# Every fourth weight chunk's lower half made by ScalarE and an adding transfer

## The chip, the cores and the metric

One core of one Trainium2 chip. The metric is the device time of one execution in microseconds. The core has a matrix engine (TensorE, PE in the profile, with its weight loads as PEld), a vector engine (VectorE, DVE), an activation engine (ScalarE, ACT), GpSimd (POOL) and SyncE (SP). Transfers run on 16 DMA engines; SP, ACT and POOL issue them from queues of their own.

## The reference

A small decoder trunk over 256 tokens of width 2048 in float32: one layer with a dilated-mixture attention, one layer with a gated sum of compressed, selected and windowed attention, and in each layer an MLP of width 8192 and a gated embedding branch. Cut to the top:

```python
for i in range(DEPTH):                      # DEPTH = 2
    hn = rmsnorm(h, attn_norm_g[i])
    if i < N_A_LAYERS:
        h = h + dilated_mixture_attention(hn, a_w_in[i], a_w_out[i])
    else:
        shared = nsa_shared_kv(rmsnorm(h, kv_norm_g), w_kv_shared, ...)
        h = h + nsa_attention(hn, b_w_qg[j], b_w_out[j], *shared)
    hn = rmsnorm(h, mlp_norm_g[i])
    h = h + jnp.square(jax.nn.relu(hn @ mlp_w1[i])) @ mlp_w2[i]
    gate = jax.nn.sigmoid(rmsnorm(h, ple_norm_g[i]) @ ple_w_gate[i])
    h = h + (p[i] @ ple_w_proj[i]) * gate
return rmsnorm(h, final_norm_g)
```

Nearly all of the work is the products with the float32 weight matrices. Each weight is used once, for 256 tokens.

## The kernel before, in words

All weights lie in HBM as *chunks* of 128 partitions by 1024 float32 values, 512 KB each, in the order in which they are used. A float32 product is made of products in float32r, a rounded form that TensorE takes: a weight chunk `raw` is split into `hi` (its rounded copy) and `lo` (what the rounding left), and the activations are split in the same way. One tile of 128 by 128 weights then takes two matmuls (`mm_tile`, lines 319 and 320): `hi` times both halves of the activations (512 columns), and `lo` times the upper half alone (256 columns). A chunk holds eight such tiles.

Where a chunk goes depends on the stage. `quad` (most stages: attention output, MLP, gate, shared keys) collects four output blocks over eight chunks; `single` (queries and keys) collects one block over two chunks; `token_major` (values) uses the weights as the streamed side (lines 402 to 404); `compress` feeds the compression MLP with its chunks interleaved with a value unit's. What comes out of a group is finished by small operations on ScalarE and VectorE: `sum_halves` (lines 324 and 326), `split_to` (430 and 432), `renorm`, `add_to_x` (435 and 436), the softmax of the two attentions.

The order of the work is written out by hand. `Program` holds a list of steps, either a chunk with the function that uses it or a plain operation. `Program.run` goes through the list, and for the chunk `at` it emits, in this order: loads as far as the raw buffers allow (`DMA_AHEAD`, `RAW_BUFS`), rounded copies up to `at + ahead + 1`, subtractions up to `at + ahead`, one step of every operation in progress (`advance`), and then the chunk's matmuls. `ahead` is `SPLIT_AHEAD` after the first chunks. Each engine runs its own instructions in the order in which they were emitted.

Four queues carry the chunk: SyncE issues its load (line 185), ScalarE makes `hi` by a copy that rounds (line 197), VectorE makes `lo = raw - hi` (line 203), TensorE reads both. There are 4 raw, 6 hi and 5 lo buffers; an engine that writes a buffer waits until the last reader of its old contents is done. The very first chunk is handled in two pieces.

GpSimd has little to do: four loads of the per-layer embeddings (`load_p`, line 484), and at the start of layer B, in `start1` (lines 748 to 774), a few memsets and small loads of tables into memory that the earlier layer gives up.

Of the kernel before, what the change touches and what calls it, by code (L numbers as in the profile page):

```python
# [13 lines left out]
ALU = mybir.AluOpType  # L14
# [17 lines left out]

WARM_UP = 7
DMA_AHEAD = 7
SPLIT_AHEAD = 3
RAW_BUFS, HI_BUFS, LO_BUFS = 4, 6, 5

G_ATTN, G_MLP, G_PLE, G_KV, G_FIN = 0, 2, 4, 6, 7

# [1 line left out]
def f32(ap):  # L41
    return ap.bitcast(F32)


class Program:
# [53 lines left out]
    def run(self, load, copy, sub):  # L99
        srcs = [s for s, _ in self.steps if s is not None]  # L100
        raw, hi, lo = {}, {}, {}
        loaded = at = copied = subbed = 0
        for src, fn in self.steps:
            if src is None:
                g = fn()
                if g is not None:
                    self.begin(g)
                continue
            starting = at < KT // 2
            if starting:  # L110
                self.advance()
            ahead = max(0, min(SPLIT_AHEAD, at - KT // 2 + 2))
            while loaded < len(srcs) and loaded <= at + DMA_AHEAD:
                if loaded >= RAW_BUFS and loaded - RAW_BUFS >= subbed:
                    break
                raw[loaded] = load(loaded, srcs[loaded])
                loaded += 1
            while copied < loaded and copied <= at + ahead + (ahead > 0):
                hi[copied] = copy(copied, raw[copied])
                copied += 1  # L120
            while subbed < copied and subbed <= at + ahead:
                lo[subbed] = sub(subbed, raw.pop(subbed), hi[subbed])
                subbed += 1
            if not starting:
                self.advance()
            self.waiting += fn(hi.pop(at), lo.pop(at)) or []
            self.finish_tensor()
            at += 1
        self.until(lambda: not self.active and not self.waiting)
# [3 lines left out]
def kernel(ctx: ExitStack, tc: tile.TileContext, a: dict, out: bass.AP):  # L133
    nc = tc.nc
# [55 lines left out]
    def pieces(n):  # L190

        return [slice(0, CH // 2), slice(CH // 2, CH)] if n == 0 else [slice(0, CH)]
# [4 lines left out]
            nc.scalar.copy(hi[:, c], t[:, c])  # L197
        return hi

    def sub(n, t, hi):  # L200
        lo = wpool.tile([P, CH], F32R, tag="lo", name="wlo", bufs=LO_BUFS)
        for c in pieces(n):
            nc.vector.tensor_sub(lo[:, c], t[:, c], f32(hi)[:, c])  # L203
        return lo
# [928 lines left out]
    ple(1, p1, x_p1, n_p1, None, n_fin, True)  # L1133

    prog.run(load, copy, sub)
    close_pool("h")

# [96 lines left out]
```

## Time and profile before

| | |
|---|---|
| median of two runs | 2530.66 us (2530.20 and 2531.12) |
| profiled execution, first to last instruction | 2529.0 us (the page gives its span only) |
| TensorE busy | 2511.8 us, 99% |
| TensorE weight loads | 2219.4 us, 88% |
| VectorE busy | 1718.4 us, 68% |
| ScalarE busy | 1329.4 us, 53% |
| GpSimd busy | 10.5 us |
| moved by DMA | 466.27 MB, mean 184 GB/s |

The profile is taken from one execution. "Busy" is time in which an engine executes an instruction; weight loads overlap matmuls. A group's row names the line, engine and operation, the tile written and the tiles read, the shapes, the count, then the busy time in us and the mean of one in ns, and after a second bar the idle time of the engine just before these instructions with what ended it. In the rows of waits, the name left of the arrow waited for the one right of it; `mm` and `at` are TensorE's two sets of result banks. A DMA issue row ends with the median time from issue to landing.

### The profile page before, as it was taken

The numbers are of one execution on the slowest core, as the hardware profiler recorded it, in microseconds if no ns is written. First come the engines' busy times: TensorE is split into PE (matmuls) and PEld (weight loads), VectorE is DVE, ScalarE is ACT, GpSimd is POOL, SyncE is SP. The second block draws the span as 40 slices with busy tenths as digits, with TensorE's granted clock in tenths as the row PEclk, the third lists the DMA queues.
The fourth block names the chain that finished last, engine by engine and source line by source line (L and its number), as shares of the span: only waits on it lengthen the run. The fifth ranks groups of instructions, "written<-read, shape, count | busy, mean of one in ns | idle before, by whom it ended". The sixth has DMA issues, their size and how long they took to land.

```text
span 2529.0 us, 38529 instructions
## 1 busy us (share of the span) xinstructions
PE 2511.8 (99%) x14717; PEld 2219.4 (88%) x14717; DVE 1718.4 (68%) x3035; ACT 1329.4 (53%) x2066; POOL 10.5 (0%) x22
## 2 busy tenths in 40 slices
PE   9999999999999999999999999999999999999997
PEld 7888888888888888888888899988888888888887
DVE  6766677866566565566788988766656656556777
ACT  6444444564354453455665777655435445445555
POOL 0000000000000000000000000000000000000000
PEclk9999999999999999999999999999999999999999
DMA  7555555566666666666566743456666666666653
GB/s 262 175 175 178 174 164 179 175 187 189 191 191 191 188 190 190 191 191 189 183 199 189 254 150 114 134 188 187 190 190 191 191 188 189 190 191 191 189 186 118
DMA packets 129690, 466.27 MB, mean 184 GB/s; under 512 B 14560, under 2 KB 15328, under 8 KB 129504
## 3 DMA queue, kind: packets, MB, share of 16 engines
q1 hardware_dynamic: 128112, 461.50, 59.2%
q8 instruction: 115, 1.88, 0.3%
q0 software_dynamic: 528, 1.07, 0.2%
q10 hardware_dynamic: 864, 1.25, 0.1%
q14 instruction: 71, 0.58, 0.1%
HBM read 461.65 MB, written 2.10 MB: 183 GB/s over the span
## 4 chain that ended last, share of the span: by engine, by line
PE 99%; DVE 0%; DMA 0%; ACT 0%; issue 0%; ACTq 0%; DVEq 0%
PE mm L319 29%; PE at L319 26%; PE mm L320 15%; PE at L320 13%; PE mm L402 1%; PE mm L404 1%; PE mm L403 1%; PE mm L374 1%; PE mm L376 1%; PE mm L375 1%; PE at L402 1%; PE at L403 1%; PE at L404 1%; PE at L1081 1%; PE mm L1103 1%; PE at L637 0%
## 5 line engine op out<-in xcount | busy, mean ns | idle before, releaser
L203 DVE TENSOR_TENSOR wlo<-raw,whi 128x1024 fp32r<-128x1024 f32 (+1 forms) x874 | 1065.1, 1220 | 622.8 <-PE at L320 242.1
L197 ACT CAST whi<-raw 128x1024 fp32r<-128x1024 f32 (+1 forms) x874 | 919.9, 1053 | 911.6 <-PE at L319 410.0
L319 PE MATMUL mm<-xa,whi 128*128 128x512 f32 x1920 | 672.8, 394 | 0.0
L319 PE MATMUL at<-xa,whi 128*128 128x512 f32 x1648 | 573.6, 392 | 0.0
L320 PE MATMUL mm<-xa,wlo 128*128 128x256 f32 x1920 | 536.4, 279 | 0.0
L320 PE MATMUL at<-xa,wlo 128*128 128x256 f32 x1648 | 461.1, 280 | 0.0
L319 PEld LDWEIGHTS mm<-xa,whi 128*128 128x128 f32 x1920 | 359.7, 187 | 81.3
L319 PEld LDWEIGHTS at<-xa,whi 128*128 128x128 f32 x1648 | 308.3, 187 | 68.0
L320 PEld LDWEIGHTS mm<-xa,wlo 128*128 128x128 f32 x1920 | 362.2, 189 | 0.4
L319 PE MATMUL at<-h,whi 128*128 128x512 f32 x1024 | 355.7, 391 | 0.0
L319 PE MATMUL mm<-h,whi 128*128 128x512 f32 x1024 | 355.7, 391 | 0.0
L320 PEld LDWEIGHTS at<-xa,wlo 128*128 128x128 f32 x1648 | 311.3, 189 | 0.1
L320 PE MATMUL mm<-h,wlo 128*128 128x256 f32 x1024 | 286.7, 280 | 0.0
L320 PE MATMUL at<-h,wlo 128*128 128x256 f32 x1024 | 286.7, 280 | 0.0
L319 PEld LDWEIGHTS at<-h,whi 128*128 128x128 f32 x1024 | 191.5, 187 | 42.0
L319 PEld LDWEIGHTS mm<-h,whi 128*128 128x128 f32 x1024 | 191.5, 187 | 42.0
L320 PEld LDWEIGHTS mm<-h,wlo 128*128 128x128 f32 x1024 | 193.5, 189 | 0.0
L320 PEld LDWEIGHTS at<-h,wlo 128*128 128x128 f32 x1024 | 193.5, 189 | 0.0
L326 DVE TENSOR_TENSOR et<-mm,es 128x256 f32<-128x256 f32 x121 | 49.1, 421 | 81.6 <-ACT es L324 79.5
L324 ACT COPY es<-mm 128x256 f32<-128x256 f32 x121 | 42.6, 372 | 68.4 <-PE mm L320 65.3
L374 PE MATMUL mm<-xa,whi 128*128 128x256 f32 x256 | 73.5, 287 | 0.0
L376 PE MATMUL mm<-xa,wlo 128*128 128x256 f32 x256 | 72.4, 283 | 0.0
(295 smaller groups left out, 2688.9 us busy)
## 6 DMA issues: line engine op xcount, KB each, us to landing
raw<-in_w SPq DMA_DIRECT2D x512, 512.0 KB, 4.3
raw<-in_w_qk SPq DMA_DIRECT2D x96, 512.0 KB, 3.6
raw<-in_w_gate SPq DMA_DIRECT2D x56, 512.0 KB, 4.0
raw<-in_w_kv SPq DMA_DIRECT2D x48, 512.0 KB, 4.3
raw<-in_w_v SPq DMA_DIRECT2D x47, 512.0 KB, 3.5
raw<-in_w_q SPq DMA_DIRECT2D x32, 512.0 KB, 4.2
raw<-in_w_oB SPq DMA_DIRECT2D x32, 512.0 KB, 3.5
raw<-in_w_oA SPq DMA_DIRECT2D x16, 512.0 KB, 3.6
```

Of the source, the lines that this page charges most:

```text
L197: nc.scalar.copy(hi[:, c], t[:, c])
L203: nc.vector.tensor_sub(lo[:, c], t[:, c], f32(hi)[:, c])
L319: nc.tensor.matmul(ps, hi[:, col:col + P], rhs, start=first, stop=False)
L320: nc.tensor.matmul(ps[:, :T], lo[:, col:col + P], rhs[:, :T], start=False, stop=last)
L324: nc.scalar.copy(s, ps[:, :T])
L326: nc.vector.tensor_add(t, ps[:, T:], s)
L374: nc.tensor.matmul(ps, wh, xg[:, :T], start=k == 0, stop=False)
L375: nc.tensor.matmul(ps, wh, xg[:, T:], start=False, stop=False)
L376: nc.tensor.matmul(ps, wl, xg[:, :T], start=False, stop=k == KT - 1)
L402: nc.tensor.matmul(st[j], xh, wh, start=k == 0, stop=False)
L403: nc.tensor.matmul(st[j], xl, wh, start=False, stop=False)
L404: nc.tensor.matmul(st[j], xh, wl, start=False, stop=k == KT - 1)
```

## The change

For chunk numbers above 20 that divide by four, `lo` is no longer made by VectorE. ScalarE writes the negated chunk, rounded, into the `lo` tile (`-hi`), and GpSimd then issues a transfer that adds the chunk to it, reading the chunk from HBM a second time: `lo = -hi + raw`. The raw tile in SBUF is not read by that transfer. For all other chunks nothing changes in how `lo` is made. Besides this, the split runs one chunk further ahead (`SPLIT_AHEAD` 4), with one more hi and one more lo buffer, and the space for GpSimd's transfer descriptors is set to 4096.

```diff
 WARM_UP = 7
 DMA_AHEAD = 7
-SPLIT_AHEAD = 3
-RAW_BUFS, HI_BUFS, LO_BUFS = 4, 6, 5
+SPLIT_AHEAD = 4
+RAW_BUFS, HI_BUFS, LO_BUFS = 4, 7, 6
...
             while subbed < copied and subbed <= at + ahead:
-                lo[subbed] = sub(subbed, raw.pop(subbed), hi[subbed])
+                lo[subbed] = sub(subbed, raw.pop(subbed), hi[subbed], srcs[subbed])
                 subbed += 1
...
-    def sub(n, t, hi):
+    def sub(n, t, hi, src):
         lo = wpool.tile([P, CH], F32R, tag="lo", name="wlo", bufs=LO_BUFS)
+        if n > 20 and n % 4 == 0:
+            nc.scalar.mul(lo, t, -1.0)
+            nc.gpsimd.dma_start(lo, src, accum_op=ALU.add)
+            return lo
         for c in pieces(n):
             nc.vector.tensor_sub(lo[:, c], t[:, c], f32(hi)[:, c])
         return lo
...
-    nc = _bacc.Bacc("TRN2", target_bir_lowering=False, num_devices=1)
+    nc = _bacc.Bacc("TRN2", target_bir_lowering=False, num_devices=1, dynamic_dma_scratch_size=4096)
```

## The prediction

> **What bounds the kernel now.** I read the page first: the busy times and the chain of work that ended last.
>
> ```profile
> span 2529.0 us, 38529 instructions
> ...
> PE 2511.8 (99%) x14717; PEld 2219.4 (88%) x14717; DVE 1718.4 (68%) x3035; ACT 1329.4 (53%) x2066; POOL 10.5 (0%) x22
> ...
> PE 99%; DVE 0%; DMA 0%; ACT 0%; issue 0%; ACTq 0%; DVEq 0%
> ```
>
> TensorE is busy in all but 2529.0 - 2511.8 = 17.2 us, and the last chain is 99% TensorE. The engine that the change relieves, VectorE, idles a third of the span. A busy PE need not be PE at its peak, so the list of TensorE's own waits comes next (waiting line, then what it waited for; us in total, times, longest).
>
> ```profile
> PE at L402 <- ACT whi L197: 3.1, 1, 3.1
> PE at L235 <- DVE sq L221: 2.2, 1, 2.2
> PE at L258 <- DVE diag L254: 1.8, 1, 1.8
> PE mm L569 <- DVE ones L168: 1.1, 1, 1.1
> ```
>
> Four waits, 8.2 us, each once; three belong to the first load (L402, L569) or the final norm (L235, L258) and none names `wlo`, the half that the change makes in another way. TensorE never waits for a weight half once it has started. The third view is the table of stretches: would TensorE run faster beside a quieter VectorE or DMA?
>
> ```profile
> core 0: us, PE busy (x) PEld busy (x) DVE busy (x) ACT busy (x) POOL busy (x), PEclk, DMA share, GB/s
> 1320.00:1340.00 20.00, 20.00 (x118) 17.51 (x117) 15.02 (x33) 9.96 (x16) 0.00 (x0) 1.00 0.54 169
> 1340.00:1360.00 20.00, 20.00 (x117) 17.51 (x116) 16.58 (x35) 10.07 (x15) 0.00 (x0) 1.00 0.66 205
> ...
> 1400.00:1420.00 20.00, 20.00 (x108) 17.28 (x107) 19.42 (x34) 13.27 (x21) 0.00 (x0) 1.00 0.89 294
> 1420.00:1440.00 20.00, 20.00 (x106) 16.35 (x104) 19.15 (x40) 18.30 (x36) 0.00 (x0) 1.00 0.75 244
> 1440.00:1460.00 20.00, 20.00 (x116) 16.97 (x116) 19.13 (x35) 16.46 (x31) 0.00 (x0) 1.00 0.86 274
> ```
>
> In the first two rows the matmul count is 118 and 117, while VectorE goes from 15.02 to 16.58 us and DMA from 169 to 205 GB/s: the rate doesn't follow them, at a granted clock of 1.00. So the gain that any help with weights can bring is bounded by the 17.2 us, 0.7%, and most of that lies at the two ends, which this edit doesn't touch (it starts at chunk 24). The last three rows are the tightest stage (the interleaved compress and value chunks): VectorE at 96%, ScalarE up to 18.30 of 20 us, DMA share up to 0.89. TensorE still shows 20.00.
>
> **The change part by part.** The groups of the loops touched, and two small groups for a price:
>
> ```profile
> L203 DVE TENSOR_TENSOR wlo<-raw,whi 128x1024 fp32r<-128x1024 f32 x872 | 1063.8, 1221 | 622.8 <-PE at L320 242.1 <-PE mm L320 203.3 <-issue 80.2
> L197 ACT CAST whi<-raw 128x1024 fp32r<-128x1024 f32 x872 | 918.8, 1054 | 911.6 <-PE at L319 410.0 <-PE mm L319 375.7 <-PE mm L403 40.2
> ...
> L464 ACT ACTIVATE et<-et 128x256 f32<-128x256 f32 x128 | 52.8, 413 | 0.0
> L430 ACT CAST h<-et 128x256 fp32r<-128x256 f32 x128 | 52.1, 407 | 4.1
> ```
>
> 872 whole chunks and the split first one make 873, numbered 0 to 872. Those above 20 that divide by four are 24 to 872, that is 213.
>
> *Removed:* 213 subtractions by 1.22 us = 260 us of VectorE, none of it on the last chain. Gain: 0.
>
> *Added on ScalarE:* 213 negated copies. The trace has none of this size; the cast of the same tile takes 1.054 us, and at 256 columns an ACTIVATE takes 413 against a cast's 407 ns, so 1.06 us: 226 us, ScalarE from 53% to 61%. Where this lies is read from the steady rhythm (ScalarE's casts, then VectorE's subtraction).
>
> ```profile
> 1000.85 1.05 ACT L197 CAST whi<-raw 128x1024 fp32r<-128x1024 f32 x1 [1.72 <-PE mm L319]
> 1003.62 1.06 ACT L197 CAST whi<-raw 128x1024 fp32r<-128x1024 f32 x1 [1.72 <-PE mm L319]
> ...
> 1023.03 1.05 ACT L197 CAST whi<-raw 128x1024 fp32r<-128x1024 f32 x1 [1.72 <-PE at L319]
> ```
> ```profile
> 1001.02 1.23 DVE L203 TENSOR_TENSOR wlo<-raw,whi 128x1024 fp32r<-128x1024 f32 x1 [1.55 <-PE mm L320]
> ```
>
> One chunk takes (1023.03 - 1000.85) / 8 = 2.77 us. Cast and subtraction start when TensorE leaves an old chunk and frees its buffer; ScalarE then idles 1.72 us. The negated copy goes into that hole every fourth chunk (1.06 of 1.72 us). In the tight stage the hole is smaller: 1420 to 1440 moved 244 GB/s x 20 us = 4.9 MB, some 9.3 chunks, so 2.3 copies, 2.5 us on top of 18.30: ScalarE would be 0.8 us over there and catches up in the next row (16.46). I take +0.8 us, bounds 0 and 2.5.
>
> *Look-ahead and buffers:* seven hi, six lo buffers with a look-ahead of four: the buffer waited for is that of chunk n-6 for chunk n instead of n-5, so both halves wait for the same moment of TensorE as before, and every half has one chunk, 2.77 us, more before it is needed. Cost 0, gain 0, since no wait on a half is there to shorten.
>
> *Added on the DMA engines:* 213 transfers that read the chunk from HBM again (213 x 0.524 = 112 MB) and add it to the tile.
>
> ```profile
> q1 hardware_dynamic: 128112, 461.50, 59.2%
> ...
> raw<-in_w SPq DMA_DIRECT2D x512, 512.0 KB, 4.3
> ...
> ps<-in_pT POOLq DMA_DIRECT2D x4, 128.0 KB, 2.6
> ```
>
> A plain chunk occupies the 16 engines for 0.592 x 2529.0 / 873 = 1.71 us, and lands 4.3 us after issue. No adding transfer is in the trace. Below, it can't be cheaper than a plain one, 1.71 us, as it moves the same bytes into the same tile; above, I take a plain pass each for reading the chunk, reading the tile and writing it, 5.1 us. I take two passes, 3.4 us: nearest to the raw load's row, with twice the bytes read. Four chunks of TensorE are 4 x 2.77 = 11.1 us; four raws fill 6.84 of it, which leaves 4.25 us. So 1.7 and 3.4 are hidden in the steady stages and 5.1 is not.
>
> The Trainium skill, *Collectives: The Full Stack*, section "The bandwidth ceiling: the fold count and why AG ≠ RS ≠ AR", says that a DMA which adds costs two reads on one read ring, so about half the rate of a copy; no run here shows an adding transfer yet. By that page it would be 2 x 1.71 = 3.4 us and the sum below the same (an estimate); the rule speaks against the change in the tight stage alone.
>
> In the tight stage the mean share is (0.89 + 0.75 + 0.86) / 3 = 0.83. One transfer more per four chunks makes it 0.83 x 1.25 = 1.04 at a plain price, x 1.5 = 1.25 at two passes, x 1.75 = 1.46 at three: 2.5, 15 or 27 us too much over 60 us. Against it stands the slack of the adding transfer (5 us, below) and four raw buffers at some 1.9 us of TensorE each (60 us by 31 chunks), 8 us. So 0, 2 or 14 us; I take 2.
>
> *Latency.* Chunk n's buffer comes free five chunks, 13.9 us, before n is needed. Cast and negated copy take 2.1 us, so 11.8 us are left for Pool's issue and the landing. Landing: 4.3 us if plain, 4.3 + 2 x 1.71 = 7.7 us with three passes; 6 us with two. Hidden with about 5 us to spare, somewhat less where the copies of finished sums stand ahead of it on ScalarE at the end of a group.
>
> *GpSimd's queue.* It now carries 213 issues, and its waits matter: whatever stands at its head holds all adding transfers behind it.
>
> ```profile
> L484 POOL DMA_DIRECT2D ps<-in_pT x4: 536/542/670, 429.9 to 1694.1; - x4
> ```
> ```profile
> 1203.44 0.96 POOL L748 MEMSET vc<- 128x1024 f32 x1 [772.12 <-PE at L320]
> ...
> 1313.12 0.31 POOL L758 MEMSET pc<- 128x256 f32 x1 [26.85 <-DVE et L527]
> ...
> 1317.82 0.56 POOL L774 DMA_DIRECT2D pe_v<-in_pe_v  x1
> ```
>
> An issue of 128 rows takes 0.54 us: 213 of them are 115 us, 5% of Pool. The waits before L748 and L758 are long because Pool reached them early; their releasers stand earlier in the program than the adding transfers queued behind them, so they cost at most the rest of that earlier work. The setup of layer B (five memsets, nine small loads, about 8.4 us of issue in all) can hold one adding transfer back by 8.4 - 2.8 = 5.6 us, once, against 5 us of slack: up to 0.6 us, taken as 0.
>
> *SyncE's queue.*
>
> ```profile
> SPq L185 <- DVE wlo L203: 1633.7, 679, 9.4
> ```
>
> A raw load waits for the subtraction that empties its buffer; for every fourth it will wait for ScalarE's negated copy, which ends 2.1 us after the release instead of 1.4 us (1001.02 + 1.23 - 1000.85). 0.7 us later, before a look-ahead of several chunks: 0.
>
> Sum: 2529.0 + 0.8 + 2 = 2531.8 us of span. The runs' median, 2530.66, lies 1.7 us above the profiled span; so 2533.5, say 2534 us.
>
> **The rivals.** What a measurement of this kernel can't tell from no change is taken as 2%, 51 us.
>
> *The DMA engines become the bound (slower).* Place: every group of four chunks from 24 on. It decides where the adding transfer takes over 4.25 us of the 16 engines, 2.5 plain ones. At three passes the group takes 6.84 + 5.13 = 11.97 us instead of 11.08: 0.89 x 213 = 190 us, 2724 us. For it: the DMA share is already 0.6 on average, and nothing in the trace prices an add. Against it: part of that share is latency (294 GB/s were moved at 0.89, so a full share is some 330 GB/s, 1.59 us a chunk). Chance 0.13, of which 0.11 over 2%.
>
> *The engines keep up but the half lands late (slower).* It decides at 11.8 us from copy to landing. A stall also widens the next one's window, so each us beyond costs half a us, 213 times: 107 us; a landing of 13 us gives 2534 + 128 = 2662. For it: raw loads on the same engines, and Pool's unseen ring. Against: 2.6 us for Pool's 128 KB. Chance 0.07, of which 0.06 over 2%.
>
> *It doesn't do what it says:* the smaller descriptor space makes Pool send a chunk in pieces, one after another. Four pieces at the 2.6 us of `ps` are 10.4 us, still hidden; six are 15.6, 3.8 late, 203 us: 2737. Chance 0.02.
>
> *A gain:* the idle of TensorE shrinks; at most 17.2 us, 2513, and none of its waits names `wlo`. Chance 0.03, within 2%.
>
> **How the numbers follow.** Forecast 0.75, with its own range 2528 to 2550 (costs of 0 to 14 us in the tight stage and 2.5 us on ScalarE, and the spread of the runs). Slower by over 2%: 0.11 + 0.06 + 0.02 = 0.19. Faster by over 2% needs more than all idle time of TensorE: 0.02 for what I can't see, taken from the forecast. The rest, 0.79, is no change. The range of 8 in 10 is 2526 to 2580: the forecast and the milder ends of the two slow rivals.
>
> **What would show it.** Right: TensorE still 99% busy with no wait naming `wlo` or the DMA, 661 subtractions, 213 copies of about 1.06 us on ScalarE, VectorE at some 58%, the software queue at 213 chunks, a landing under 8 us, and any new TensorE idle between 1400 and 1460 us. Wrong: TensorE waiting for a DMA every fourth chunk with landings over 11 us (late), or a DMA share near 1 in the steady slices with raw loads late as well (the engines full), or matmuls that start further apart without a wait, which would mean that the extra traffic slows TensorE itself.

## The result, and the profile after

The changed kernel takes 2553.8 us (median of 2552.6 and 2555.0) against 2530.66 us: 1.0091 times as long, interval 1.0062 to 1.012. That is 23 us more, inside the range of 2526 to 2580 and within the 2% taken as no change, but above the 2528 to 2550 that I gave the likeliest case by itself, and 20 us above the point.

The page of the kernel after: the span, the busy times, the last chain's engines, the two queues that matter (packets, MB, share of 16 engines) and the adding transfers (KB each, us to landing).

```profile
span 2553.2 us, 38987 instructions
...
PE 2519.4 (99%) x14717; PEld 2222.6 (87%) x14717; DVE 1468.2 (58%) x2822; ACT 1517.2 (59%) x2279; POOL 195.0 (8%) x235
...
q1 hardware_dynamic: 128112, 461.50, 54.5%
q0 software_dynamic: 31200, 112.75, 24.2%
...
PE 93%; DMA 4%; issue 1%; DVE 1%; ACT 1%; POOL 0%; ACTq 0%; DVEq 0%; POOLq 0%
...
wlo<-in_w POOLq DMA_DIRECT2D x128, 512.0 KB, 7.4
```

VectorE is relieved as meant, 68% to 58%, and the time grew all the same: the last chain, 99% TensorE before, now holds 4% of DMA. TensorE's busy time grew by 7.6 us and its idle time from 17.2 to 33.8 us. TensorE's own waits of the kernel after name the place (four rows of the kernel before are still there):

```profile
PE mm L860 <- DMA wlo<-in_w_c: 11.1, 5, 4.4
PE at L406 <- ACT whi L197: 3.0, 1, 3.0
PE mm L324 <- DMA wlo<-in_w: 2.7, 1, 2.7
...
PE at L239 <- DVE acc L231: 1.1, 1, 1.1
...
PE at L324 <- DMA wlo<-in_w_gate: 1.0, 1, 1.0
PE mm L324 <- DMA wlo<-in_w_kv: 0.4, 1, 0.4
```

Five waits of 213 adding transfers carry 11.1 us: those of `w_c`, the compression MLP's chunks. The stretches show the contrast between a uniform stage, the kernel before and then the kernel after, and that one in the kernel after (columns as in the prediction):

```profile
600.00:640.00 40.00, 40.00 (x233) 35.28 (x232) 23.17 (x31) 14.79 (x14) 0.00 (x0) 1.00 0.60 187
```
```profile
600.00:640.00 40.00, 40.00 (x233) 35.24 (x232) 19.01 (x27) 18.90 (x19) 3.46 (x4) 1.00 0.80 232
...
1400.00:1420.00 20.00, 15.58 (x77) 13.27 (x76) 13.98 (x31) 12.12 (x19) 1.73 (x2) 0.91 0.93 272
1420.00:1440.00 20.00, 18.89 (x101) 15.70 (x100) 11.21 (x20) 13.40 (x24) 1.73 (x2) 1.00 0.85 245
1440.00:1460.00 20.00, 15.67 (x82) 12.53 (x81) 16.45 (x39) 16.79 (x30) 1.73 (x2) 1.00 0.90 277
```

In the MLP the DMA share went from 0.60 to 0.80 and TensorE lost nothing: 233 matmuls in 40 us, as before. In the compress and value stage TensorE lost 20.00 - 15.58 = 4.4 us in the first 20 us, and the granted clock of the row is 0.91 (more in the last section).

Both kernels execute the same 14717 matmuls in the same order, so the delay of the n-th one against the kernel before says where time was lost. This table, made from the start times in the traces, is used for all runs (us lost in each part; parts are named by their times in the kernel before). Each row is one profiled execution.

```
                    0-479  479-1242 1242-1380 1380-1482 1482-1700 1700-1770 1770-2463 2463-2520   sum
                    A      MLP 0    gate, kv  compress  heads     MLP 1 in  MLP 1     gate, end
the change           0.5    0.0      2.1      13.8       0.0       6.0       0.0       1.2       23.7
the change again     0.2    0.0      0.9      14.1       0.0       4.6      -0.1       1.2       20.9
e1 stage             0.1    0.0      1.7       3.9       0.0       0.3       0.0       1.7        7.6
e2 embeddings       -0.5    0.0      1.3      14.8       0.0       0.0       0.1       1.5       17.2
e13 embeddings      -0.9    0.0      2.9      14.9       0.0       0.0       0.1       2.9       20.0
e3 both             -0.5    0.0      0.9       6.2       0.0       0.0       0.0       2.1        8.7
e4 look-ahead        0.1    0.0      0.0       0.0       0.0       0.0       0.0       0.0        0.1
e5 every second      0.0   33.8      8.1      34.4      -0.1      15.4      28.8       2.5      123.0
e6 plain copy       -0.8    0.0      0.0       5.8       0.1       0.0       0.0       0.0        5.2
e7 every third       0.3   17.9      2.9      24.4      -0.3       0.8      -0.1       1.9       47.7
e10 spare tile       0.7    0.0      1.7       7.9       0.0       0.8      -0.2       2.4       13.3
e11 long stages     -0.7    0.0      0.0       0.0       0.0       0.0       0.0       0.0       -0.6
e14 stage alone     -0.1    0.0      0.0      14.9       0.0       0.0       0.0       0.0       14.9
```

The change lost 13.8 us in the compress stage, 6.0 us at the beginning of the second MLP, 3.3 us around the two gate branches, and nothing in some 1400 us of MLP.

### The profile page after: what moved, and what is told of

The parts are those of the page before. It is cut to its first block, busy times and chain, and to the rows that moved or that the text cites. A ratio compares the mean times of both kernels' runs of the same rounds, so it can differ in the third digit from the quotient of the medians.

```text
span 2553.2 us, 38987 instructions
## 1 busy us (share of the span) xinstructions
PE 2519.4 (99%) x14717; PEld 2222.6 (87%) x14717; DVE 1468.2 (58%) x2822; ACT 1517.2 (59%) x2279; POOL 195.0 (8%) x235
## 3 DMA queue, kind: packets, MB, share of 16 engines
q0 software_dynamic: 31200, 112.75, 24.2%
## 4 chain that ended last, share of the span: by engine, by line
PE 93%; DMA 4%; issue 1%; DVE 1%; ACT 1%; POOL 0%; ACTq 0%; DVEq 0%; POOLq 0%
PE mm L323 28%; PE at L323 24%; PE mm L324 15%; PE at L324 13%; PE mm L406 1%; PE mm L408 1%; PE mm L407 1%; PE mm L378 1%; PE mm L380 1%; PE mm L379 1%; DMA wlo<-in_w_c 1%; DMA raw<-in_w 1%; PE at L1085 1%; PE at L406 1%; PE at L407 1%
## 5 line engine op out<-in xcount | busy, mean ns | idle before, releaser
L207 DVE TENSOR_TENSOR wlo<-raw,whi 128x1024 fp32r<-128x1024 f32 (+1 forms) x661 | 805.2, 1219 | 703.3 <-PE at L324 293.1
L324 PE MATMUL mm<-xa,wlo 128*128 128x256 f32 x1920 | 537.5, 280 | 3.0 <-DMA wlo<-in_w 2.7
L203 ACT ACTIVATE wlo<-raw 128x1024 fp32r<-128x1024 f32 x213 | 224.8, 1055 | 0.0
L204 POOL DMA_DIRECT2D wlo<-in_w x128 | 110.7, 865 | 1314.9 <-ACT wlo L203 915.9
L330 DVE TENSOR_TENSOR et<-at,es 128x256 f32<-128x256 f32 x103 | 43.3, 422 | 80.4 <-ACT es L328 75.0
```

The source lines that it names most:

```text
L203: nc.scalar.mul(lo, t, -1.0)
L204: nc.gpsimd.dma_start(lo, src, accum_op=ALU.add)
L324: nc.tensor.matmul(ps[:, :T], lo[:, col:col + P], rhs[:, :T], start=False, stop=last)
L330: nc.vector.tensor_add(t, ps[:, T:], s)
```

## The experiments

**The two places.** Four kernels, each starting from the change. The stage: VectorE makes the halves of chunks 484 to 515 again.

```diff
-        if n > 20 and n % 4 == 0:
+        if n > 20 and n % 4 == 0 and not 484 <= n < 516:
```

> Theory: 14 of the 24 us come from the eight adding transfers in the interleaved compress and value stage (chunks 484 to 515), so with VectorE making those eight halves again the kernel takes about 2554 - 14 = 2540 us, and TensorE waits for no transfer of w_c. Rival (the loss is spread: a fuller DMA, a busier ScalarE or slower matmuls everywhere): eight of 213 transfers fewer give back 1 us, 2553.

Measured 2541.71 us, 1.0042 times the kernel before (1.0027 to 1.0057): 12 of 23 us come back for eight transfers of 213. No wait for a `w_c` transfer is left. The stage still loses 3.9 us, with a wait of 2.3 us for a small copy that I had not expected; it stands below with e3.

The embeddings: the change issues the two small loads of layer 1's embeddings from GpSimd right behind an adding transfer. GpSimd's and then ScalarE's rows of the kernel after (start, duration; idle time before and its releaser in brackets):

```profile
1716.11 0.87 POOL L204 DMA_DIRECT2D wlo<-in_w  x1 [10.96 <-ACT wlo L203]
1716.65 1.44 POOL L488 DMA_DIRECT2D ps<-in_pT  x2
```
```profile
1715.73 1.03 ACT L197 CAST whi<-raw 128x1024 fp32r<-128x1024 f32 x1
1726.49 0.41 ACT L434 CAST pg<-ps 128x256 fp32r<-128x256 f32 x1 [9.74 <-DMA ps<-in_pT]
```

The load that landed in 2.6 us before (median) now needs longer; the row of `ps` in the kernel after:

```profile
DMA to landing us min/median/max: 7.3/8.7/10.1
```

ScalarE takes its instructions in order, so for 9.74 us it makes no rounded copy. In this part TensorE has two waits of the list above, 1.1 us for the norm's sum (`acc`) and 2.7 us for an adding transfer of `in_w`. e2 sends these loads through SyncE.

```diff
-            nc.gpsimd.dma_start(s, a["pT"][layer][:, k * T:(k + 1) * T])
+            nc.sync.dma_start(s, a["pT"][layer][:, k * T:(k + 1) * T])
```

> Theory: the loads of the per-layer embeddings stand behind an adding transfer in GpSimd's queue, land 9.7 us after ScalarE begins to wait for them, and cost 6 us near 1740 us; issued from SyncE instead, they land before they matter: 2554 - 6 = 2548 us. Rival (those 6 us come from the fuller DMA or from the adding transfers themselves, and the wait for the embeddings is hidden): no change, 2554.

> The change itself once more, as the partner of the next run on the same chip: 2554, 2551 to 2557.

> The change with the loads of the embeddings issued from SyncE, beside the change itself. Theory (that wait costs about 6 us of TensorE in every execution): 6 us under the run before it. Rival (it costs them only in executions in which the raw loads happen to be late at that place, since with a wait of 5.8 us instead of 9.7 us TensorE lost 0.2 us there): 0 to 3 us under it.

First 2551.85 us (1.0080, interval 1.0065 to 1.0095); in the pair on one chip 2551.68 us with the edit and 2552.28 us for the change itself (1.0085, 1.0071 to 1.0098, against 1.0081, 1.0068 to 1.0094). That is 0.6 us less where the theory of the last expectation had 6. In the profiled executions the place behaves as the theory says: 6.0 and 4.6 us lost with the load on GpSimd, 0.0 both times on SyncE. But e1 kept it on GpSimd and lost 0.3 us there, with ScalarE waiting 5.8 us instead of 9.7. This suggests that the wait costs TensorE only where it is long enough to use up the halves made in advance. In the profiled execution of e13 the gate parts lost 2.9 us each instead of 0.9 and 1.2. The mechanism is seen in the traces; a gain in the median is not shown.

> Theory: the two places are independent, so both edits together give 2554 - 14 - 6 = 2534, within 4 us of the kernel before, although 205 adding transfers remain. Rival (spread loss): above 2545.

2539.66 us, 1.0031 (1.0018 to 1.0043): neither 2534 nor above 2545. Of the 205 transfers left, one stands just behind the stage, at chunk 516, and the profiled execution of e3 shows what it does. ScalarE's rows, then TensorE's:

```profile
1453.70 1.05 ACT L197 CAST whi<-raw 128x1024 fp32r<-128x1024 f32 x1
1458.82 1.05 ACT L197 CAST whi<-raw 128x1024 fp32r<-128x1024 f32 x1 [4.07 <-DMA raw<-in_w_q]
1459.78 0.37 ACT L870 COPY et<-mm 128x256 f32<-128x256 f32 x1
```
```profile
1460.19 1.12 PE L874 MATMUL mm<-et,pair 128*64 128x256 f32 x2 [3.34 <-ACT et L870]
```

ScalarE waits 4.07 us for a raw load that is late beside the adding transfer; a small copy of the GELU stands behind it in ScalarE's order, and TensorE waits 3.34 us for that copy. So there is a second way to lose time, through a late raw load and not through a late half. That the transfer of chunk 516 makes the load late is read from the order of events; no run leaves out that one alone.

> Look-ahead and buffers alone, no adding transfer and no negated copy. Theory: no wait on a weight half existed, so no gain and no cost: 2531 us within 2. Rival: the deeper look-ahead itself moves work on ScalarE and VectorE and brings part of the loss, 2535 or more; or it gains, below 2527.

```diff
-        if n > 20 and n % 4 == 0:
+        if n < 0:
```

2530.90 us, 1.0000 (0.9991 to 1.0010); matmul for matmul the two traces differ by 0.1 us. Look-ahead, buffers and descriptor space cost nothing and bring nothing.

**What the adding costs.** e6 leaves out the add, and so part of the computation.

```diff
-            nc.gpsimd.dma_start(lo, src, accum_op=ALU.add)
+            nc.gpsimd.dma_start(lo, src)
```

> The transfer copies the chunk into the tile instead of adding it (the lower half then holds the whole chunk, so the values are not the reference's; count, bytes from HBM, negated copy and waits are as in the change). Theory (the add, with its second read, makes the landing long, and that costs the time in the tight stage): occupancy falls from 2.88 to about 1.7 us, the landing from 7.4 to about 5.5 us, and most of the loss goes: 2540 or less. Rival (any second transfer of 512 KB, or the 226 us of negated copies on ScalarE, costs the time): 2550 or more.

2539.21 us, 1.0035 (1.0021 to 1.0050). The software queue and the landing in e6:

```profile
q0 software_dynamic: 31200, 112.75, 12.5%
...
wlo<-in_w POOLq DMA_DIRECT2D x128, 512.0 KB, 4.6
```

TensorE's wait for the transfers of `w_c` in e6, and the landing of the software queue's transfers between 1383 and 1467 us:

```profile
PE mm L860 <- DMA wlo<-in_w_c: 4.6, 4, 1.4
```
```profile
DMA to landing us min/median/max: 4.6/5.8/6.8
```

The same packets and bytes take 12.5% instead of 24.2%: 0.125 x 2534.7 / 213 = 1.49 us of the 16 engines for a copy, 0.242 x 2553.2 / 213 = 2.90 us for an add, 1.95 times as much. They land in 4.6 instead of 7.4 us. In the profiled execution, the shortest of e6's five, all places but the compress stage lose nothing, and that loses 5.8 instead of 13.8 us. By the medians some 15 of the 23 us are thus the add (2553.8 against 2539.21); the negated copies on ScalarE, present in both, cost nothing outside that stage in the trace.

**More of them.**

```diff
-        if n > 20 and n % 4 == 0:
+        if n > 20 and n % 2 == 0:
```

> Every second chunk above 20 instead of every fourth: 426 adding transfers. From the changed kernel's queue shares a raw load occupies the engines for 0.545 x 2553.2 / 873 = 1.59 us and an adding transfer for 0.24 x 2553.2 / 213 = 2.88 us. Two chunks of TensorE are 5.55 us, two raws and one adding transfer 6.07 us. Theory (these shares are true occupancy, so the engines become the bound here and weren't at every fourth): 0.52 x 426 = 222 us more than before, near 2755, with TensorE waiting in all stages. Rival (the shares contain latency that overlaps, the engines are not full): below 2600.

2653.75 us in a single execution, between the two. A stretch of the MLP in e5, and its queues:

```profile
800.00:900.00 100.00, 96.42 (x548) 83.53 (x548) 34.43 (x54) 55.83 (x65) 14.64 (x17) 1.00 1.00 276
```
```profile
q1 hardware_dynamic: 128112, 461.50, 51.3%
q0 software_dynamic: 61872, 224.44, 44.7%
```

The DMA share is 1.00 and TensorE waits in a uniform stage for the first time. By e5's own shares a raw load takes 0.513 x 2652.0 / 873 = 1.56 us and an add 0.447 x 2652.0 / 426 = 2.78 us, so two raws and an add need 5.90 of 5.55 us: 0.35 x 426 = 149 us. Measured: 123 us, of which the two long MLPs have 62.6 and the tight places much of the rest, while part A lost nothing; so the sum is confirmed in kind and not to the microsecond. The bound by occupancy is there, the shares from the less loaded kernel overstated it (5.90 instead of 6.07 us), and 222 us was too much.

> Every third chunk: 284 adding transfers. Three raws and one adding transfer are 3 x 1.59 + 2.88 = 7.65 us of 8.32 us of TensorE. Theory (a bound by occupancy, reached between every third and every second): the steady stages stay hidden, and the loss grows only with the count in the tight places, 23 x 284 / 213 = 31 us, near 2562. Rival (landing time is the limit, and the window of five chunks is used up by it earlier): above 2600.

2578.63 us in a single execution, instead of 2562 (`n % 3`). The tight stage lost 24.4 us. The 17.9 us in the first MLP surprised me: TensorE's only waits there, two at its beginning, make 3.9 us. The last section takes it up.

**Bandwidth or window in the stage.** The transfers of the stage go into a tile that nobody reads.

```diff
+        if n % 4 == 0 and 484 <= n < 516:
+            nc.gpsimd.dma_start(spare, src, accum_op=ALU.add)
-        if n > 20 and n % 4 == 0:
+        elif n > 20 and n % 4 == 0:
```

> In the compress and value stage the adding transfers go into a spare tile that nobody reads, without a negated copy, and VectorE makes the eight halves; elsewhere as in the change. Theory A (in the stage TensorE waits because the half lands after its window): the loss goes as it did without those transfers, 2542. Theory B (in the stage the DMA engines are full and raw loads come late as well): the loss stays, 2548 or more. A value between says both.

2545.29 us, 1.0059 (1.0044 to 1.0074): between the two, and by the expectation that says both. The stage loses 7.9 us, of 13.8 with the halves needed and 3.9 without the transfers. TensorE's longest wait in e10:

```profile
PE mm L878 <- ACT et L874: 5.9, 2, 4.7
```

It is the GELU's copy again, the way through late raw loads. By subtraction, some 4 of the 10 us that e1 regained go with the transfers' traffic and some 6 with the half being needed. This division is rough. It is made from single profiled executions, e10 also leaves out the eight negated copies on ScalarE, and each of its transfers waits for the one before it, as both write the same tile (53 us of GpSimd's time in seven waits), so they don't start when those of the change do. In the change itself TensorE's waits in the stage all name a `w_c` transfer.

**Each part alone.** Only the eight transfers of the stage, and only those of the long uniform stages (153 of 213 by the trace's count; the expectation says 151).

```diff
-        if n > 20 and n % 4 == 0:
+        if n % 4 == 0 and 484 <= n < 516:
```

> Adding transfers only for the eight chunks 484, 488 to 512 of the compress and value stage; VectorE makes all other halves. Theory (this stage alone loses the time, whatever happens elsewhere): 2530 + 14 = 2544, TensorE waiting for w_c transfers for some 11 us. Rival (the loss there needs the backlog that earlier adding transfers leave in the DMA queues): 2535 or less.

```diff
-        if n > 20 and n % 4 == 0:
+        if n % 4 == 0 and (20 < n < 144 or 170 <= n < 416 or 590 <= n < 837):
```

> Adding transfers only in the three long uniform stages (first attention's projections, chunks 24 to 143; the two MLPs, 170 to 415 and 590 to 836), 151 of 213; VectorE makes the others. Theory (in a uniform stage of 2.77 us a chunk the transfer is hidden, and the loss belongs to the places where chunks are short or a norm has to be finished): within 2 us of the kernel before, 2531 to 2533. Rival (each adding transfer costs a little everywhere, 23 / 213 = 0.11 us): 2531 + 16 = 2547.

Eight transfers alone: 2546.72 us, 1.0064 (1.0047 to 1.0081), 14.9 us lost and all of it in the stage, with TensorE waiting at the same line:

```profile
PE mm L860 <- DMA wlo<-in_w_c: 9.4, 4, 3.9
```

So the stage needs no backlog from elsewhere. The 153 of the long stages: 2530.95 us, 1.0012 (1.0002 to 1.0023), nothing lost in any part of the profiled execution; its eleven executions lay between 2529.99 and 2542.21 us, and what the longest two lost was not in a trace. This kernel has some seven tenths of the change's adding transfers at a median within 1 us of the kernel before; none of the versions beats that kernel, since TensorE has nothing to gain.

## Why the prediction was right or wrong

*The forecast as a whole: no change, as forecast, but not by the mechanism expected.* The time lies in the range of 2526 to 2580 because that range had room for the milder ends of the slow rivals. Of the signs of being right, the busy share, the counts and the idle time between 1400 and 1460 us came true; "no wait naming `wlo` or the DMA" did not.

*What bounds the kernel: right.* TensorE did not profit from a quieter VectorE, and e4 and e11 repeat the time of before to within 1 us. (All four of the waits listed there, not three, belong to the first load or the final norm.)

*VectorE and ScalarE: right.* 661 subtractions and 58% as forecast; the negated copy took 1.055 us (1.06 forecast), ScalarE is at 59% (61%). The 0.8 us taken for ScalarE in the tight stage don't show: it is busy at most 16.79 of 20 us there.

*Look-ahead: right*, shown by e4.

*The price of the add: the value near, the landing a little short.* I took 3.4 us of the engines between bounds of 1.7 and 5.1; measured 2.90. The landing was 7.4 us (6 taken, 7.7 the upper bound; the longest took 10.4 us). The steady stages hide it, as forecast. The Trainium skill, *Collectives: The Full Stack*, section "The bandwidth ceiling: the fold count and why AG ≠ RS ≠ AR", has the adding transfers of a collective at about half the rate of copies because an add reads two sources. The trace agrees: 1.95 times a copy's 1.49 us.

*The rival of full engines: its condition did not hold here, and holds with more transfers.* At every fourth chunk 4 x 1.59 + 2.90 = 9.3 us of 11.1 are used; at every second the DMA share is 1.00 and TensorE waits.

*The tight stage: the step that failed.* I found it, put the overload at 15 us and the upper bound at 14 us, and took 2, because I set against it "the slack of the adding transfer (5 us, below)" and four raw buffers. The slack was worked out with chunks of 2.77 us (13.9 us for five, 11.8 after the copies). In this stage 31 chunks take 60 us, 1.94 us each: five are 9.7 us, and 7.6 us after the cast and the negated copy. One adding transfer of the kernel after, from ScalarE's copy over GpSimd's issue to TensorE:

```profile
1404.92 1.05 ACT L197 CAST whi<-raw 128x1024 fp32r<-128x1024 f32 x1 [1.96 <-DMA raw<-in_w_kv]
1405.87 1.06 ACT L203 ACTIVATE wlo<-raw 128x1024 fp32r<-128x1024 f32 x1
```
```profile
1407.22 0.86 POOL L204 DMA_DIRECT2D wlo<-in_w_c  x1 [10.19 <-DVE wlo L207]
```
```profile
1411.58 0.28 PE L859 MATMUL mm<-whi,z 128*128 128x256 f32 x1
1416.28 0.45 PE L860 MATMUL mm<-wlo,z 128*128 128x256 f32 x1 [4.42 <-DMA wlo<-in_w_c]
```

From the copy's end (1406.93) to TensorE's go-ahead 9.4 us pass, 0.3 us to GpSimd and 9.0 us of issue and landing. The window has 7.6 us at best, and here the copy itself began late because ScalarE had waited 1.96 us for a raw load: TensorE came to the chunk at 1411.58 us, 4.7 us after the copy's end. So a short window and a late start of the copy meet. e6 shows that the landing alone is not all of it: its transfers land in 4.6 to 6.8 us in this stage, inside the 7.6 us, and TensorE still waits 4.6 us for them. The same slack was, besides, subtracted from a sum that already had every engine at its limit. Measured: 13.8 us. That the upper bound of 14 us lies near it is luck: it was worked out for an add of 5.1 us, less the same slack, and the add took 2.90 us.

*GpSimd's queue: a cost of 0 that was not 0.* I looked at what the older instructions could hold back, the adding transfers behind them, and not at the reverse: the embedding loads behind an adding transfer, with ScalarE waiting in order for them: 6.0 us in the profiled execution, though without these waits the median fell by only 0.6 us.

*Late landing as a rival: its mechanism came true, in a few places only.* I had priced it for all 213 transfers. The waits for late halves stand mostly where the chunks are short (11.1 us for `w_c`, 4.1 us for all others).

The sum by the terms of the profiled execution: 13.8 + 6.0 + 3.3 + 0.5 = 23.6 us in place of 2.8. Of the 3.3 us around the gates only 1.4 are waits for adding transfers (`in_w_gate`, `in_w_kv`); the cause of the rest stays open.

## What to carry to other kernels

A look-ahead is counted in chunks but a transfer takes microseconds: work out the window with the chunk time of the shortest stage, not of the longest, and never set a slack from one stage against a load in another. When a new kind of transfer enters a queue, list also what will stand behind it, and which engine waits in order for that. And an engine at 68% is no reason for an edit when another one is at 99% with no wait on it: here the best the edit could do was to cost nothing.

## What the runs showed of the hardware that was not expected

*TensorE has a second, slower rhythm.* In e7 the same loop runs at two rates at a granted clock of 1.00, without any wait:

```profile
600.00:640.00 40.00, 40.00 (x228) 34.71 (x227) 18.25 (x26) 19.85 (x20) 4.29 (x5) 1.00 0.90 250
...
1900.00:1940.00 40.00, 40.00 (x233) 34.93 (x232) 17.08 (x25) 19.94 (x20) 3.73 (x5) 1.00 0.93 257
```

228 matmuls in 40 us against 233, 2%. It began after two stalls, TensorE's only waits in the first MLP of e7, near 510 and 520 us:

```profile
PE at L239 <- DVE acc L231: 2.5, 1, 2.5
PE at L324 <- DMA wlo<-in_w: 1.4, 1, 1.4
```

It held for some 700 us through two layers of matrices and was gone after the gate branch. It makes some 13 of the 17.9 us of e7's first MLP, and the two stalls the rest. The DMA share is about the same in both rows, so the traffic of that moment does not explain it. If the stalls set it off, which was not tested, a stall can cost more than its length. Whether it also makes the spread of these kernels' executions (2537.95 to 2545.89 us in e1, against 2530.12 to 2531.71 us for the kernel before beside it) was not tested, nor what ends it.

*After some stalls the granted clock is halved for a moment.* Three stretches of 3.4 us in the kernel after:

```profile
1416.50:1419.90 3.40, 3.40 (x12) 2.96 (x12) 1.80 (x5) 2.09 (x2) 0.00 (x0) 0.50 1.00 305
1744.10:1747.50 3.40, 3.40 (x12) 2.84 (x11) 0.00 (x0) 0.33 (x2) 0.00 (x0) 0.51 0.89 264
1445.00:1448.40 3.40, 3.13 (x17) 2.77 (x18) 2.48 (x5) 3.40 (x5) 0.86 (x1) 1.00 0.56 217
```

The first follows the 4.4 us wait that ends at 1416.28 us. Seven matmuls of 256 columns start about 0.21 us apart there instead of 0.12, and five of 512 columns 0.42 us instead of 0.23: some 1.7 us on top of the wait. With the 11.1 us of waits, that makes most of the stage's 13.8 us. The second comes 1.4 us after a wait of 2.7 us ends, in the part with the embeddings, and is some of the 6.0 us lost there. The third follows a wait of 2.75 us and has the full clock. So the length of one wait does not decide it, and what does was not tested.
